# A Strassen matmul with logsumexp: two of eight row tiles taken out of the plain first column block, transposed by DMA instead of PE, and done at the end by seven products

## The chip, the cores and the metric

The kernel runs on one core of one Trainium2 chip. The metric is the device time of one execution in microseconds (us), as the median of several executions. A profile (trace) is one such execution; its span is some 2 us shorter than its time.

Names: PE is the tensor engine, PEld its weight load, DVE the vector engine, ACT the scalar engine, POOL the GpSimd engine, and SP the sync engine, which here only issues DMAs.

## The reference

```python
a = np.random.randn(1024, 4096).astype(np.float32)
b = np.random.randn(4096, 4096).astype(np.float32)

def reference(a, b):
    x = np.matmul(a, b)
    return special.logsumexp(x, axis=-1).astype(np.float32)
```

## The kernel before

The result has 8 row tiles of 128 rows and 8 column blocks of 512 columns. The inputs are cast to f16 by the DMAs that load them.

Column block 0 is done by plain 128x512 products while `a` streams in: PE transposes each 128x128 piece of `a`, DVE and ACT copy the transposes from PSUM (the tensor engine's accumulators) into `aT`, and DVE makes the sums `s1`, `s2`, `s5` of pieces of `a` that Strassen's method needs (called early sums), and two more in place (late sums, `a21-a11` and `a12-a22`), once the plain products have read the originals. Of PSUM's eight tiles, six hold the accumulators of row tiles 0 to 5 and two the transposes, so row tiles 6 and 7 come last. This is the order in which `a` (and, in between, block 0 of `b`) arrives:

```python
    for kn in (4,) * 8:
        ...
        for m in range(MT - 2):                      # row tiles 0 to 5, in rounds of four pieces
            arrivals.append((k0, kn, "a", m))
            if m < kn // 2:
                arrivals.append((k0 + 2 * m, 2, "b", k0))
    for kc in range(KC):
        for m in range(MT - 2, MT):                  # row tiles 6 and 7, after all of the others
            arrivals.append((kc * JT, JT, "a", m))
```

Column blocks 1 to 7 are done by one level of Strassen-Winograd. Two row tiles (a pair `q`) times 512 columns make one "quad" of four 128x256 results and take seven products M1 to M7 of 16 matmuls each, 112 matmuls. Five sums of each block of `b` are made by DVE, called T1, T3, T4, T6, T7. Cut to its core:

```python
            m1(c11, start=True); m5(c12)
            nc.scalar.copy(out=e, in_=r0...)         # r0 is the PSUM tile of c11 and c12
            m2(c21, start=True); m6(c22)
            nc.scalar.copy(out=s[:, 2], in_=c21)
            flush()                                  # exponentials of the quad before
            if tail:                                 # last quad of a block: sums for the next
                for g in range(G):
                    nxt.do_t1(g)
            add(s[:, 2], s[:, 2], e[:, 1])
            sub(s[:, 0], s[:, 2], e[:, 0])
            if final:                                # very last quad
                ...
                combine(0, m0, NB)                   # rows 0-5: the parts of all blocks put together
                sub(lg[:, 0:m0], lg[:, 0:m0], nmmin[:, 0:m0])
                m3(c12)
                nc.scalar.copy(out=x0, in_=c12)
                m4(c21); m7(z, start=True)           # z: the last product
                lse_max(c12, m0, nb); ...            # maxima, exponentials, logarithm, store
                continue
            if tail:
                ...                                  # T6, T3 of the next block
            m7(c11); m3(c12)
            nc.scalar.copy(out=x[:, 0], in_=c12)
            m4(c21)
            nc.scalar.copy(out=x[:, 1], in_=c21)
            ...                                      # results put together
            if tail:
                ...                                  # T4, T7 of the next block
            for h in range(2):
                lse_max(rows[h], 2 * q + h, nb)      # row maxima; exponentials go to the next flush()
```

Of the kernel before, what the change touches and what calls it, by code (L numbers as in the profile page):

```python
# [13 lines left out]
def kernel(  # L14
# [7 lines left out]
    P = 128  # L22
# [13 lines left out]
    SC = 1024  # L36
    KC, JT = K // SC, SC // P
    G = 4
    GI = KP // G
    assert (MT, KT, NB) == (8, 32, 8) and JT == 2 * GI and KC == G  # L40

    a_m = a.rearrange("(p mt) k -> mt p k", mt=MT)

    cst_pool = ctx.enter_context(tc.tile_pool(name="cst", bufs=1))
    bt_pool = ctx.enter_context(tc.tile_pool(name="btp", bufs=2 * G))
    fix_pool = ctx.enter_context(tc.tile_pool(name="fix", bufs=1))
    psum_pool = ctx.enter_context(
# [22 lines left out]
    T1, T4, T6 = tb[:, 0], tb[:, 1], tb[:, 2]  # L70
# [8 lines left out]
    lg = cst_pool.tile([P, MT], f32, name="lg")  # L79

# [47 lines left out]
    def load_b(nb, g, parts=1):  # L128
        bt = bt_pool.tile([P, GI, 2, FD], f16, name=f"b_{nb}_{g}", tag="bt")
        step = 2 * GI // parts  # L130
        flat = bt.rearrange("p i t n -> p (i t) n")
        rows = b.rearrange("(k p) n -> p k n", p=P)
        for h in range(parts):
            nc.gpsimd.dma_start(  # L134
                out=flat[:, h * step : (h + 1) * step],
                in_=rows[:, g * 2 * GI + h * step : g * 2 * GI + (h + 1) * step, ts(nb, FD)],
            )
        return bt

    class Block:  # L140
        def __init__(self, nb):
            self.nb, self.raw = nb, []
# [4 lines left out]
        def rawg(self, g, kp, h):  # L147
            return self.raw[g][:, :, kp, ts(h, H)]

        def do_t1(self, g):  # L150
            add(T1[:, ts(g, GI)], self.rawg(g, 0, 0), self.rawg(g, 1, 1))

        def do_t4(self, g):
            sub(T4[:, ts(g, GI)], self.rawg(g, 1, 0), self.rawg(g, 0, 0))

        def do_t6(self, g):
            add(T6[:, ts(g, GI)], self.rawg(g, 0, 0), self.rawg(g, 0, 1))

        def do_t7(self, g):
            add(self.rawg(g, 1, 0), self.rawg(g, 1, 0), self.rawg(g, 1, 1))  # L160

        def do_t3(self, g):
            sub(self.rawg(g, 0, 1), self.rawg(g, 0, 1), self.rawg(g, 1, 1))
# [5 lines left out]
    blk0 = Block(0)  # L169
# [76 lines left out]
    rounds = []  # L246
    for kn in (4,) * 8:
        k0 = sum(rounds)
        rounds.append(kn)
        for m in range(MT - 2):  # L250
            arrivals.append((k0, kn, "a", m))
            if m < kn // 2:
                arrivals.append((k0 + 2 * m, 2, "b", k0))
    for kc in range(KC):
        for m in range(MT - 2, MT):
            arrivals.append((kc * JT, JT, "a", m))
# [4 lines left out]
    def behind(k0, kn, what, x):  # L261

        if what == "a":
            have_a.setdefault(k0, []).append(x)
            todo = [(k, x) for k in range(k0, k0 + kn) if k in have_b]
        else:
            have_b.update({k0: 1, k0 + 1: 1})
            todo = [(k, m) for k in (k0, k0 + 1) for m in have_a.get(x, [])]
        for k, m in todo:
            if m == MT - 2 and k == 0:  # L270
                acc.append(acc_tiles("l"))
            plain(acc[m // 2][m % 2], k // 2, k % 2, m)
        r = slice(k0 // 2, (k0 + kn) // 2)
        if what == "a" and x < MT - 2:
            if x >= 3 and len(in_place) >= 3:
                a_sums_late(*in_place.pop(0))
            if x % 2 == 1:
                a_sums_early(r, x // 2)
            if x == 5:
                in_place.extend([(r, 0), (r, 1), (r, 2)])  # L280
        if what == "a" and k0 + kn == KT and x in (4, 5):
            first_max(2 * x - 8)
            first_max(2 * x - 7)
        if what == "a" and x >= MT - 2:
            n = 2 * (k0 // JT) + x - (MT - 2)
            if n < 2:
                first_max(4 + n)
            elif in_place:
                a_sums_late(*in_place.pop(0))
# [8 lines left out]
    blk = Block(1)  # L298

    def load(k0, kn, what, x):  # L300
        if what == "a":
            load_a(k0, kn, x)
            return
        if k0 % JT == 0:
            blk0.raw.append(bt_pool.tile([P, GI, 2, FD], f16, name=f"b_0_{k0}", tag="bt"))
        nc.gpsimd.dma_start(  # L306
            out=blk0.raw[k0 // JT][:, k0 % JT // 2],
            in_=b[k0 * P : (k0 + 2) * P, ts(0, FD)].rearrange("(t p) n -> p t n", p=P),
        )

    coming = list(arrivals)
    back = []
    for n, (k0, kn, what, x) in enumerate(arrivals):
        while coming and (coming[0][2] == "b" or loads[0] < count[0] + NSLOT):
            load(*coming.pop(0))
            if len(coming) == len(arrivals) - 3:
                make_identity(nc, ident)
                nc.gpsimd.memset(negmax, 3.0e38)
                nc.gpsimd.memset(tsum, 0.0)
        if not coming and not blk.raw:  # L320
            for g in range(G):
                blk.raw.append(load_b(1, g))
        if what == "a":
            transpose_group(k0, kn, x)
        if k0 < rounds[0] and x < 3:
            warm(1)
        if len(back) == min(3, 1 + n // 8):
            behind(*back.pop(0))
        back.append((k0, kn, what, x))
    while back:  # L330
        behind(*back.pop(0))

    for g in range(G):
        if g == 2:
            for m in range(MT - 2, MT):
                first_max(m)
        for f in (blk.do_t1, blk.do_t6, blk.do_t4, blk.do_t7, blk.do_t3):
            f(g)
# [9 lines left out]
    for nb in range(1, NB):  # L348
        nxt = None
        if nb + 1 < NB:  # L350
            nxt = Block(nb + 1)
            for g in range(G):
                nxt.raw.append(load_b(nb + 1, g))
        quads = {}
        for q in range(MP):
            if q not in quads:

                both = (0, 1) if nb == 1 and q == 0 else (q,)
                for p in both:
                    quads[p] = acc_tiles(f"{nb}_{p}")  # L360
# [4 lines left out]
            def product(c, lhs, rhs, start=False, g=None):  # L365
                for i in range(KP) if g is None else range(g * GI, (g + 1) * GI):
# [9 lines left out]
            first, tail = nb == 1 and q < 2, nxt is not None and q == MP - 1  # L376
            final = nxt is None and q == MP - 1
# [4 lines left out]
            s = fix_pool.tile([P, 4, H], f32, name=f"s_{nb}_{q}", tag="s")  # L382
            x, e = s[:, 1::2], s[:, 0:2]
            if final:
                e = fix_pool.tile([P, 2, H], f32, name=f"e_{nb}_{q}", tag="e")
            if first and q == 1:
                e = e1

            def m1(c, p=q, **k):
                product(c, lambda i: s1[:, i, p], lambda i: T1[:, i], **k)  # L390
# [7 lines left out]
            def m6(c, p=q, **k):  # L398
                product(c, lambda i: aT[:, i, 0, p, 1], lambda i: T6[:, i], **k)
# [7 lines left out]
            def m4(c, **k):  # L407
                product(c, lambda i: aT[:, i, 1, q, 1], lambda i: T4[:, i], **k)

            if first and q == 0:  # L410
                for g in range(G):
                    for p in both:
                        u0, u1 = quads[p]
                        m1(u0[:, 0:H], p=p, start=True, g=g)
                        m5(u0[:, H:FD], p=p, g=g)
                        m2(u1[:, 0:H], p=p, start=True, g=g)
                        m6(u1[:, H:FD], p=p, g=g)
            elif not first:
                m1(c11, start=True)
                m5(c12)  # L420
            if not (first and q == 1):
                nc.scalar.copy(out=e, in_=r0.rearrange("p (h n) -> p h n", h=2))  # L422
            if not first:
                m2(c21, start=True)
                m6(c22, start=final)
            nc.scalar.copy(out=s[:, 2], in_=c21)  # L426
            flush()
            if first and q == 0:
                e1 = fix_pool.tile([P, 2, H], f32, name=f"e_{nb}_1", tag="e")
                nc.scalar.copy(out=e1, in_=quads[1][0].rearrange("p (h n) -> p h n", h=2))  # L430
            if tail:
                for g in range(G):
                    nxt.do_t1(g)
            add(s[:, 2], s[:, 2], e[:, 1])
            sub(s[:, 0], s[:, 2], e[:, 0])
            if final:
# [4 lines left out]
                combine(0, m0, NB)  # L441
                sub(lg[:, 0:m0], lg[:, 0:m0], nmmin[:, 0:m0])
# [30 lines left out]
            if tail:  # L473
                for f in (nxt.do_t6, nxt.do_t3):
                    for g in range(G):
                        f(g)
# [9 lines left out]
            if tail:  # L486
                for f in (nxt.do_t4, nxt.do_t7):
                    for g in range(G):
                        f(g)
# [3 lines left out]
            if first and q == 1:  # L493
                a_sums_early(slice(0, KP), MP - 1)
                a_sums_late(slice(0, KP), MP - 1)
        blk = nxt
# [32 lines left out]
```

## Time and profile before

| | before |
|---|---|
| time | 429.63 us, median of 4 (428.7 to 430.32) when predicting; 429.18 us, median of 15 with later runs |
| span of the profile | 427.1 us |
| PE | 98% busy, 92% of the chain that ended last |
| plain 128x512 product, one after another | 0.216 us |
| 128x128 transpose | 0.055 us |
| 128x256 product | 0.109 us; a quad of 112: 12.225 us |
| first Strassen product starts | 80.11 us |
| last product ends | 422.62 us; 4.48 us before the end |

From the profile page: busy times, the DMA's busy share in 40 slices of the span, and the chain that ended last, by engine.

```profile
PE 418.5 (98%) x3663; PEld 347.9 (81%) x3663; DVE 233.6 (55%) x517; ACT 112.6 (26%) x278; POOL 66.9 (16%) x108
...
DMA  8999999999009900596009910398008930000000
...
PE 92%; DMA 3%; DVE 2%; ACT 1%; issue 1%; POOL 1%; DVEq 0%; ACTq 0%; POOLq 0%
```

The chain is nearly all PE, so a microsecond of PE work should be a microsecond of time. The DMA queues have long idle stretches after the first quarter (the zeros), so there is room for more loading. PE's busy share alone would not be proof: the Trainium skill, "Trainium Kernel Development and Optimization", section "Performance Expectations", calls matmul busy time a bad metric for how close a kernel is to its roofline, because matmuls are pipelined, and names MFU (the share of the peak arithmetic rate that is used) and the busy share of the weight load as the good ones. MFU was not worked out here.

From the timeline of PE, at the change from plain to Strassen products (start, length, engine, line, operation, count).

```profile
72.76 0.61 PE L199 MATMUL tps<-ident,tb 128*128 128x128 f16 x8
73.21 7.07 PE L217 MATMUL acc_l<-b,aT 128*128 128x512 f16 x32
80.11 0.60 PE L367 MATMUL acc<-tb,s 128*128 128x256 f16 x4
```

The plain products of tiles 6 and 7 (`acc_l`) end as the first Strassen product starts. The length of a group includes the pipelined end of its last matmul, so the next group starts a little before the sum of start and length. There is no idle time (it would stand in brackets).

From the timeline of all engines, the last quad.

```profile
405.60 0.43 DVE L82 TENSOR_TENSOR s<-s 128x256 f32<-128x256 f32 x1 [4.10 <-ACT s L426]
...
410.24 1.91 PE L367 MATMUL acc<-tb,s 128*128 128x256 f16 x16
...
416.12 0.42 DVE L82 TENSOR_TENSOR s<-s,e 128x256 f32<-128x256 f32 x1 [2.40 <-ACT s L426]
...
419.57 0.42 DVE L88 TENSOR_REDUCE negmax<-acc 128x1 f32<-128x256 f32 x1 [0.48 <-ACT s L444]
...
420.71 1.91 PE L367 MATMUL z<-b,aT 128*128 128x256 f16 x16
```

The last quad starts at 410.24, and the last product, z, ends at 420.71 + 1.91 = 422.62. DVE has idle time here (4.10 and 2.40 us in brackets): no next block needs sums. The row maximum of C12 starts at 419.57. From there a chain of short operations runs to the end.

### The profile page before, as it was taken

How to read it: one execution, taken by the hardware profiler on the slowest of the kernel's cores; microseconds unless marked ns; L12 is line 12 of the kernel's file. 1: busy time of each engine (PE TensorE's matmuls, PEld its weight loads, DVE VectorE, ACT ScalarE, POOL GpSimd, SP SyncE). 2: the span in 40 equal slices, each digit the busy share in tenths (PEclk: the TensorE clock that was granted, in tenths of full speed). 3: DMA queues.
4: the chain of work that ended last, by engine and by line, in shares of the span. 5: the costliest groups of instructions: out<-in, count | busy, mean ns of one | idle time of the engine just before them, and what ended most of it. 6: DMA issues, size and time to landing. Idle time of an engine off the chain costs nothing.

```text
span 427.1 us, 8496 instructions
## 1 busy us (share of the span) xinstructions
PE 418.5 (98%) x3663; PEld 347.9 (81%) x3663; DVE 233.6 (55%) x517; ACT 112.6 (26%) x278; POOL 66.9 (16%) x108
## 2 busy tenths in 40 slices
PE   7999999999999999999999999999999999999995
PEld 2555565688888888888888888888888888888884
DVE  1456677744789324862369333863359531883235
ACT  1222335112222212222221222222212222222134
POOL 7766752100011000300003000300003000000000
PEclk9999999999999999999999999999999999999999
DMA  8999999999009900596009910398008930000000
GB/s 119 197 203 204 203 208 207 207 207 207 16 0 198 197 3 1 79 207 111 2 0 164 207 27 0 47 207 145 0 2 131 208 57 2 2 2 2 1 2 1
DMA packets 41717, 42.49 MB, mean 99 GB/s; under 512 B 1744, under 2 KB 40656, under 8 KB 41680
## 3 DMA queue, kind: packets, MB, share of 16 engines
q0 software_dynamic: 41536, 41.95, 59.9%
q8 instruction: 28, 0.46, 0.4%
q14 instruction: 9, 0.07, 0.1%
q1 hardware_dynamic: 144, 0.00, 0.0%
HBM read 83.89 MB, written 0.00 MB: 196 GB/s over the span
## 4 chain that ended last, share of the span: by engine, by line
PE 92%; DMA 3%; DVE 2%; ACT 1%; issue 1%; POOL 1%; DVEq 0%; ACTq 0%; POOLq 0%
PE acc L367 79%; PE acc L217 8%; DMA tb<-in_a_dram 3%; PE tps L199 3%; PE acc_l L217 2%; ACT acc L93 0%; DVE negmax L88 0%; PE c L367 0%; DVE aT L85 0%; POOL tb L188 0%; DVE s L82 0%; ACT aT L212 0%; POOL b L306 0%; DVE aT L210 0%; ACT s L467 0%
## 5 line engine op out<-in xcount | busy, mean ns | idle before, releaser
L367 PEld LDWEIGHTS <-aT 128*128 128x128 f16 x1792 | 175.3, 98 | 20.3
L367 PEld LDWEIGHTS <-s 128*128 128x128 f16 x1344 | 131.5, 98 | 15.4
L367 PE MATMUL acc<-tb,aT 128*128 128x256 f16 x880 | 106.0, 273 | 0.0
L367 PE MATMUL acc<-b,s 128*128 128x256 f16 x896 | 103.4, 273 | 0.0
L367 PE MATMUL acc<-b,aT 128*128 128x256 f16 x880 | 100.6, 273 | 0.0
L85 DVE TENSOR_TENSOR s<-s 128x256 f32<-128x256 f32 (+1 forms) x54 | 30.1, 557 | 85.2 <-ACT s L481 84.3
L134 POOL DMA_DIRECT2D b<-in_b_dram x28 | 24.6, 888 | 242.0 <-PE acc L367 226.6
L367 PE MATMUL acc<-tb,s 128*128 128x256 f16 x448 | 54.5, 273 | 0.0
L217 PE MATMUL acc<-b,aT 128*128 128x512 f16 x192 | 49.8, 379 | 0.0
L82 DVE TENSOR_TENSOR s<-s 128x256 f32<-128x256 f32 x26 | 11.0, 422 | 60.3 <-ACT s L426 60.3
L93 ACT ACTIVATE acc<-acc,negmax 128x512 f32<-128x512 f32 (+1 forms) x62 | 40.7, 657 | 5.1 <-DVE negmax L88 4.6
L88 DVE TENSOR_REDUCE negmax<-acc 128x1 f32<-128x512 f32 (+1 forms) x62 | 39.4, 676 | 1.2 <-ACT s L444 0.5
L422 ACT COPY s<-acc 128x512 f32<-128x512 f32 x26 | 15.2, 586 | 87.1 <-PE acc L367 87.1
L82 DVE TENSOR_TENSOR tb<-b 128x1024 f16<-128x1024 f16 x56 | 35.0, 684 | 4.2 <-DMA b<-in_b_dram 4.2
L217 PEld LDWEIGHTS <-aT 128*128 128x128 f16 x256 | 22.7, 98 | 17.5 <-ACT aT L212 0.3
L199 PEld LDWEIGHTS <-tb 128*128 128x128 f16 x256 | 18.8, 99 | 17.7 <-DMA tb<-in_a_dram 5.1
L188 POOL DMA_DIRECT2D tb<-in_a_dram x56 | 30.3, 544 | 8.8 <-PE tps L199 3.1
L212 ACT COPY aT<-tps 128x512 f16<-128x512 f16 (+1 forms) x28 | 18.1, 648 | 48.5 <-PE tps L199 48.5
L426 ACT COPY s<-acc 128x256 f32<-128x256 f32 x28 | 10.4, 372 | 74.8 <-PE acc L367 73.1
L210 DVE COPY aT<-tps 128x512 f16<-128x512 f16 (+1 forms) x28 | 12.9, 462 | 30.4 <-PE tps L199 30.4
L199 PE MATMUL tps<-ident,tb 128*128 128x128 f16 x256 | 23.7, 221 | 2.9 <-DMA tb<-in_a_dram 2.7
L82 DVE TENSOR_TENSOR acc<-acc,s 128x256 f32<-128x256 f32 x54 | 20.6, 428 | 2.7 <-DVE s L85 0.5
(51 smaller groups left out, 173.1 us busy)
## 6 DMA issues: line engine op xcount, KB each, us to landing
b<-in_b_dram POOLq DMA_DIRECT2D x28, 1024.0 KB, 17.0
tb<-in_a_dram POOLq DMA_DIRECT2D x48, 128.0 KB, 5.9
b<-in_b_dram POOLq DMA_DIRECT2D x16, 256.0 KB, 6.2
tb<-in_a_dram POOLq DMA_DIRECT2D x8, 256.0 KB, 7.4
out_dram<-lg SPq DMA_DIRECT2D x1, 4.0 KB, 1.4
```

Source lines behind the costliest of these rows:

```text
L82: nc.vector.tensor_tensor(out=o, in0=x, in1=y, op=ALU.add)
L85: nc.vector.tensor_tensor(out=o, in0=x, in1=y, op=ALU.subtract)
L88: nc.vector.tensor_reduce(out=negmax[:, m, nb : nb + 1], in_=pt, axis=AX.X, op=ALU.max, negate=True)
L93: nc.scalar.activation(out=pt, in_=pt, func=AF.Exp, bias=negmax[:, m, nb : nb + 1], scale=scale, accum_out=tsum[:, m, nb : nb + 1],)
L134: nc.gpsimd.dma_start(out=flat[:, h * step : (h + 1) * step], in_=rows[:, g * 2 * GI + h * step : g * 2 * GI + (h + 1) * step, ts(nb, FD)],)
L188: nc.gpsimd.dma_start(out=slot, in_=a_m[m, :, k0 * P : (k0 + kn) * P])
L199: nc.tensor.matmul(pst[:, ts(j, P)], src[:, ts(j, P)], ident, is_transpose=True, start=(j == 0), stop=(j == kn - 1),)
L210: nc.vector.tensor_copy(out=dst, in_=v)
L212: nc.scalar.copy(out=dst, in_=v)
L217: nc.tensor.matmul(pt, aT[:, i, kp, m // 2, m % 2, :], blk0.raw[i // GI][:, i % GI, kp, :], start=(done[m] == 0), stop=(done[m] == KT - 1),)
L367: nc.tensor.matmul(c, lhs(i), rhs(i), start=(start and i == 0), stop=(i == KP - 1), skip_group_check=True,)
L422: nc.scalar.copy(out=e, in_=r0.rearrange("p (h n) -> p h n", h=2))
```

## The change

The intent: 64 plain products are dearer than one quad (64 x 0.216 = 13.8 us against 12.2 us), and 64 transposes come on top (3.5 us). So row tiles 6 and 7 leave the first stage. They are copied to DRAM in f16, brought into `aT` by two DMA transposes on SP's queue, and block 0 and block 1 of these rows are done at the very end by one quad each ("again0", "again1"), for which both blocks of `b` are loaded once more. Block 1's other three quads are now done jointly, in eighths, as block 1 arrives. A gate, a tiny copy on POOL that reads the transposed data, keeps the load of block 3 from being issued before the transposes have landed. The combination of rows 0 to 5 moves to the quad before the last.

```diff
-    for kc in range(KC):
-        for m in range(MT - 2, MT):
-            arrivals.append((kc * JT, JT, "a", m))
...
+    again0 = lambda: Block(0, sums=[wide(t[:, :, 0:2]) for t in (s1, s2, s5)])
+    again1 = lambda: Block(1, raw=[wide(aT[:, ts(g, GI), :, 0:2]) for g in range(G)])
+    plan = [(lambda: blk1, range(MP - 1))]
+    plan += [(lambda nb=nb: Block(nb), range(MP)) for nb in range(2, NB)]
+    plan += [(again0, [MP - 1]), (again1, [MP - 1])]
...
+                if step == 1:
+                    nc.gpsimd.tensor_copy(out=gate, in_=aT[:, 0, 0, MP - 1, :, 0])
+                nxt = plan[step + 1][0]().load_all()
+        if step == 0:
+            a16 = dram_pool.tile([2, P, K], f16, name="a16")
+            for m in range(2):
+                nc.gpsimd.dma_start(out=a16[m], in_=a_m[MT - 2 + m])
+            for m in range(2):
+                nc.sync.dma_start_transpose(
+                    aT[:, :, :, MP - 1, m, :].rearrange("p i t c -> p (i t) c"), a16[m]
+                )
...
+                for lo in range(0, KP, 2):             # block 1, three quads jointly, by eighths
+                    if lo > 0:
+                        for what in ("t1", "t6"):
+                            blk.make(what, lo, lo + 2)
+                    if lo == KP - 2:
+                        while in_place:
+                            a_sums_late(*in_place.pop(0))
...
+            one = tail and len(qs) == 1
+            if one:
+                nxt.make("t1")
+                combine(0, 2 * q, NB)
+                sub(lg[:, 0 : 2 * q], lg[:, 0 : 2 * q], nmmin[:, 0 : 2 * q])
...
-                combine(0, m0, NB)
-                sub(lg[:, 0:m0], lg[:, 0:m0], nmmin[:, 0:m0])
```

## The prediction

> **What bounds the kernel now.** The tensor engine (PE), back to back. The chain of waits is 92% PE; the PE timeline has no gap between 23.7 us and the last product at 422.6 us. By the page's chain, a plain 128x512 product costs 0.216 us, a 128x128 transpose 0.055, a 128x256 Strassen product 0.109 (one group of 112, a "quad", 12.225 us). From 10.25 us: 256 plain products and 256 transposes until 80.1, then 28 quads x 12.225 = 342 us. A vector/scalar tail of about 4.5 us follows the last product (span 427.1, median 429.63).
>
> **What the change does to PE.** Row tiles 6 and 7 leave column block 0 and are never transposed on PE: 64 plain products (13.8 us) and 64 transposes (3.5 us) go, 17.3 us. One quad comes: 29 instead of 28 (rows 6-7 of block 0 done by seven products at the end). Net 5.1 us less PE work, all on the critical path. That is the whole gain, 1.2%.
>
> **What it gives back.**
> 1. Change-over to block 1. Before, the transposes and products of tiles 6-7 hid the row maxima, exponentials and sums there. Now vector work must finish first. From the timeline at 58-66 us, my estimate: last plain product at 62.4, while the vector engine still has late sums (0.48 us each pair), early sums (0.69), four row maxima (0.64 each) and then the first T1 sum, ready at about 63.7; later PE waits for the last exponentials to free PSUM. About 1.7 us of new PE idleness. Not bound by loads: block 1 no longer queues behind tiles 6-7 (about 10 us of DMA at 207 GB/s), so its eighths arrive from about 60.5 us every 2.5 us, against 2.6 us of PE per eighth.
> 2. Tail. The last step is again preceded by a quad that must make five sums for it (2.5 us each), plus the final combination of rows 0-5. By the durations at 410-424 us, the maxima and exponentials of the quad before then come late, and the scalar copy of the last C12 slips by about 1.5 us; the chain after it is pure latency, so the end slips by 1.5.
>
> **The side path.** Tiles 6-7 go to DRAM as f16 behind block 2, landing at about 106 and 111 us, then two DMA transposes of 1 MiB. The trace of before has none. The Trainium skill, "DMA: Bandwidth & Descriptors", section "Latency and other measured facts", gives 261 GB/s for a transpose with a non-contiguous middle dimension: an estimate of 4 us each. The sums want them by about 128 us and block 3's load, gated on them, by about 124. So I expect no stall, but one transpose over about 9 us would begin to cost, one for one. The reloads of blocks 0 and 1 fall into idle DMA time (the slices show zeros) and cost nothing.
>
> **Sum.** 429.6 - 5.1 + 1.7 + 1.5 = 427.7; I say 427.3, range 424.3 to 431.5. Chance of faster by over 2%: 0.04; within 2%: 0.88; slower by over 2%: 0.08.
>
> **What would show it right or wrong.** Plain products end near 62.4 instead of 73-80 us. The first Strassen product waits on the vector engine for 1-2 us. Last product ends near 419 us; 3,645 or so PE instructions; from there to the end 6 us instead of 4.5. DMA transposes land before 124 us, and PE shows no wait at the fourth quad of block 2 or the first of block 3.
>
> **What would make it wrong.** Slow DRAM writes or transposes (a stall of 5-15 us around 125-150 us, hence the slower chance); a larger stall at the change-over; or the tail's slip being absorbed (then 425).

## The result, and the profile after

| | before | after |
|---|---|---|
| time, median (lowest to highest), executions | 429.18 (428.7 to 430.32), 15 | 426.2 (425.74 to 428.1), 11 |
| ratio | 1 | 0.9933, 95% interval 0.9922 to 0.9944 |
| span of the profile | 427.1 | 424.9 |
| first Strassen product | 80.11 | 64.53 |
| from there to the start of z | 340.60 | 353.37 |
| last product ends | 422.62 | 419.81 |
| from there to the end of the span | 4.48 | 5.09 |

A ratio here is the mean time of one kernel's fast runs over that of the other's of the same rounds, so it is not quite the ratio of the medians quoted. The kernel is faster by 0.7%, which counts as the same time at a limit of 2%.

From the profile page after: the same three lines.

```profile
PE 414.1 (97%) x3647; PEld 348.5 (82%) x3647; DVE 258.1 (61%) x566; ACT 110.1 (26%) x278; POOL 73.3 (17%) x115
...
DMA  8999999999969599003980089300990059599000
...
PE 86%; DVE 7%; DMA 4%; ACT 1%; issue 1%; POOL 1%; DVEq 0%; ACTq 0%; POOLq 0%
```

PE has 16 instructions fewer: 64 products and 64 transposes went, 112 products came. DVE has 24.5 us more to do and a part in the chain, 7%. The new loads near the end fill slices that were zero.

From the timeline of PE and DVE after, at the change from plain to Strassen products.

```profile
59.79 3.62 PE L228 MATMUL acc<-b,aT 128*128 128x512 f16 x16
60.25 0.48 DVE L87 TENSOR_TENSOR aT<-aT 128x256 f16<-128x256 f16 x2
60.65 1.28 DVE L90 TENSOR_REDUCE negmax<-acc 128x1 f32<-128x512 f32 x2
...
62.86 1.28 DVE L90 TENSOR_REDUCE negmax<-acc 128x1 f32<-128x512 f32 x2
64.06 0.75 DVE L84 TENSOR_TENSOR tb<-b 128x512 f16<-128x512 f16 x2
64.53 0.39 PE L383 MATMUL acc<-tb,s 128*128 128x256 f16 x2 [1.12 <-DVE tb L84]
```

Plain products end at 63.41 us. DVE is busy without a break with late sums (L87), row maxima (L90) and early sums (L84, in the lines left out), and only then makes the first T1 (`tb`). PE waits 1.12 us for it.

From the timeline of PE and DVE after, in the first quad of block 2.

```profile
105.11 2.48 DVE L87 TENSOR_TENSOR tb<-b 128x1024 f16<-128x1024 f16 x4
107.51 2.49 DVE L84 TENSOR_TENSOR b<-b 128x1024 f16<-128x1024 f16 x4
108.25 4.15 PE L383 MATMUL acc<-b,aT 128*128 128x256 f16 x32
...
115.73 3.66 PE L383 MATMUL acc<-b,s 128*128 128x256 f16 x32
```

A group of 32 products that is not held up takes 3.66 us (the last line). The group of M7 and M3 at 108.25 took 4.15: its products follow DVE's T7 (L84, group by group) and wait 0.5 us in all. The prediction did not have this wait.

From the timeline of PE and DVE after, the last quad.

```profile
406.00 2.49 DVE L87 TENSOR_TENSOR aT<-aT 128x1024 f16<-128x1024 f16 x4
407.42 1.91 PE L383 MATMUL acc<-tb,s 128*128 128x256 f16 x16
...
412.27 2.49 DVE L84 TENSOR_TENSOR aT<-aT 128x1024 f16<-128x1024 f16 x4
...
414.68 1.28 DVE L90 TENSOR_REDUCE negmax<-acc 128x1 f32<-128x512 f32 x2
...
417.14 0.42 DVE L90 TENSOR_REDUCE negmax<-acc 128x1 f32<-128x256 f32 x1
...
417.90 1.91 PE L383 MATMUL z<-aT 128*128 128x256 f16 x16
```

DVE now makes the five sums for "again1" without a break, and the row maximum of C12 comes 9.72 us after the quad's start (417.14 - 407.42), where it was 9.33. The last product ends at 419.81, and the end follows 5.09 us later instead of 4.48. Of these 0.61 us, 0.39 are the later maximum; the operations from the maximum to the last one of DVE take the same time in both traces, and the other 0.2 us lie behind DVE's last operation (2.6 us instead of 2.4), where only the store of the result is left. Why that is longer was not looked into.

From the DMA issues (name, queue, count, median us from issue to landing), the waits of POOL, and the timeline of POOL, all after: the side path. Each is one view.

```profile
aT<-a SPq DMA_TRANSPOSE x2, 8.5
```

```profile
POOL gate L359 <- DMA aT<-a: 44.7, 1, 44.7
```

```profile
119.37 0.18 POOL L359 COPY gate<-aT 128x2 f16<-128x2 f16 x1 [44.66 <-DMA aT<-a]
119.94 3.54 POOL L144 DMA_DIRECT2D b<-in_b_dram  x4 [0.38 <-issue]
```

The transposes took 8.5 us each from issue to landing (8.7 and 8.2), twice the estimate, and the gate opened at 119.37. No PE wait followed. The moving itself was not slow: between 114 and 117 us, when the second transpose was the only transfer under way, the DMA moved 286 GB/s, at which 1 MiB takes 3.7 us. The rest of the 8.5 us lies before the first byte and after the last, or beside another transfer.

**The ledger.** The start of Strassen moved by -15.58 us: 17.3 us of work removed, 1.12 us of new waiting, and some 0.6 us of waits for the first loads that differ from run to run (below). The stretch from there to z grew by 353.37 - 340.60 = 12.77 us: one quad (12.225) and 0.54 us of waiting. The tail grew by 0.61. So -17.3 + 12.2 + 1.12 + 0.54 + 0.61 = -2.8 us without the loads. With them it is -2.2, as the two profiled spans differ. The medians differ by 3.0.

**The loads.** The last group of plain products starts at 59.79 in this trace, and in those of all ten other runs with the same loads of the first stage (the second run of this kernel, e10, and all of the experiments below but e7) at 58.69 to 60.29, as the waits for the first pieces of `a` come out shorter or longer. That spread of 1.6 us is of the size of the effects sought. So where a fraction of a microsecond matters, the text reads distances inside one execution, which do not contain it.

### The profile page after: what moved, and what is told of

Same layout as the page of the kernel before. It is cut to its first block, busy times and chain, and to the rows that moved or that the text cites. A ratio compares the mean times of both kernels' runs of the same rounds, so it can differ in the third digit from the quotient of the medians.

```text
span 424.9 us, 8520 instructions
## 1 busy us (share of the span) xinstructions
PE 414.1 (97%) x3647; PEld 348.5 (82%) x3647; DVE 258.1 (61%) x566; ACT 110.1 (26%) x278; POOL 73.3 (17%) x115
## 4 chain that ended last, share of the span: by engine, by line
PE 86%; DVE 7%; DMA 4%; ACT 1%; issue 1%; POOL 1%; DVEq 0%; ACTq 0%; POOLq 0%
PE acc L383 78%; PE acc L228 6%; DMA tb<-in_a_dram 3%; PE tps L210 2%; DMA b<-in_b_dram 1%; DVE negmax L90 1%; DVE tb L84 1%; DVE aT L87 1%; DVE s L87 1%; DVE aT L84 1%; DVE tb L87 1%; DVE s L84 0%; DVE acc L84 0%; POOL tb L199 0%; POOL b L144 0%
## 5 line engine op out<-in xcount | busy, mean ns | idle before, releaser
L383 PEld LDWEIGHTS <-s 128*128 128x128 f16 x1392 | 136.1, 98 | 17.4 <-DVE tb L84 1.6
L383 PE MATMUL acc<-tb,aT 128*128 128x256 f16 x880 | 108.5, 273 | 0.0
L144 POOL DMA_DIRECT2D b<-in_b_dram x52 | 41.9, 814 | 222.8 <-PE acc L383 207.8
L87 DVE TENSOR_TENSOR s<-s 128x512 f32<-128x512 f32 (+1 forms) x55 | 30.8, 559 | 74.6 <-ACT s L521 73.5
L84 DVE TENSOR_TENSOR s<-s 128x256 f32<-128x256 f32 x26 | 10.9, 421 | 50.9 <-ACT s L459 50.7
L90 DVE TENSOR_REDUCE negmax<-acc 128x1 f32<-128x512 f32 (+1 forms) x64 | 40.7, 676 | 0.7
L84 DVE TENSOR_TENSOR tb<-b 128x1024 f16<-128x1024 f16 (+1 forms) x64 | 36.1, 617 | 4.9 <-DMA b<-in_b_dram 2.8
L210 PEld LDWEIGHTS <-tb 128*128 128x128 f16 x192 | 14.3, 99 | 16.6 <-DMA tb<-in_a_dram 8.9
L199 POOL DMA_DIRECT2D tb<-in_a_dram x48 | 25.9, 543 | 6.2 <-issue 2.4
L221 DVE COPY aT<-tps 128x512 f16<-128x512 f16 x24 | 10.2, 424 | 25.6 <-PE tps L210 25.4
L223 ACT COPY aT<-tps 128x512 f16<-128x512 f16 x24 | 14.0, 585 | 44.5 <-PE tps L210 44.5
L84 DVE TENSOR_TENSOR acc<-acc,s 128x256 f32<-128x256 f32 x56 | 21.4, 428 | 2.4
L210 PE MATMUL tps<-ident,tb 128*128 128x128 f16 x192 | 18.9, 221 | 3.3 <-DMA tb<-in_a_dram 3.3
```

Of the source, the lines that this page charges most:

```text
L84: nc.vector.tensor_tensor(out=o, in0=x, in1=y, op=ALU.add)
L87: nc.vector.tensor_tensor(out=o, in0=x, in1=y, op=ALU.subtract)
L90: nc.vector.tensor_reduce(out=negmax[:, m, nb : nb + 1], in_=pt, axis=AX.X, op=ALU.max, negate=True)
L144: nc.gpsimd.dma_start(out=self.raw[lo // GI][:, lo % GI : lo % GI + hi - lo], in_=b_rows[:, lo:hi, :, ts(self.nb, FD)],)
L199: nc.gpsimd.dma_start(out=slot, in_=a_m[m, :, k0 * P : (k0 + kn) * P])
L210: nc.tensor.matmul(pst[:, ts(j, P)], src[:, ts(j, P)], ident, is_transpose=True, start=(j == 0), stop=(j == kn - 1),)
```

## The experiments

My theory was the prediction's: the gain is the PE work, minus DVE work that is too late at two places, the change-over and the last quad, to which the trace added the first quad of block 2; the side path is hidden. The rivals: PE work is not worth its time there; the gate or the transposes cost time; the DVE waits are not the cause of what is missing, and something else binds there.

| run | what it is | median us | ratio to before, 95% interval |
|---|---|---|---|
| e1_combine_early | combination one quad earlier | 426.05 | 0.9925 (0.9912 to 0.9937) |
| e2_late_sums_later | last late sums deferred | 425.81 | 0.9917 (0.9904 to 0.9931) |
| e3_block2_sums | two sums of block 2 earlier | 426.2 | 0.9926 (0.9913 to 0.9938) |
| e8_all_three | these three together | 425.55 | 0.9913 (0.99 to 0.9927) |
| e4_dose | 32 more products in the middle | 429.84 | 1.0006 (0.9988 to 1.0025) |
| e5_no_gate | no gate | 432.71 | 1.0077 (1.0058 to 1.0096) |
| e6_late_transposes | transposes later | 434.52 | 1.012 (1.0099 to 1.0142) |
| e7_half | before, with only the quad at the end | 442.8 | 1.0314 (1.0289 to 1.0339) |
| e9_reordered | e8 and a new order of sums and products | 426.86 | 0.9944 (0.9925 to 0.9962) |
| e10_after_again | the change, once more beside e9 | 426.51 | 0.9927 (0.991 to 0.9945) |
| e11_order_m3_m7 | e9 with the products in another order | 424.15 | 0.9892 (0.9876 to 0.9909) |

All results were correct. The kernel before took 429.07 to 429.52 us (medians), so medians can differ by 0.45 us without a cause in the kernel. The intervals of e1, e2, e3 and e8 overlap with that of the change (0.9922 to 0.9944): by time alone none of the four is told from it, and what they show is in the distances below. e11's interval lies clear of it. The distances of the profiled executions, all worked out from the timelines; "to z" is from the start of the first Strassen product to the start of z, and 29 quads without any wait would give 28 x 12.225 + 6/7 x 12.225 = 352.8:

| run | wait at the change-over | to z | from the end of z to the end |
|---|---|---|---|
| after | 1.12 | 353.37 | 5.09 |
| e1_combine_early | 1.12 | 353.38 | 5.08 |
| e2_late_sums_later | 0 | 354.23 | 5.15 |
| e3_block2_sums | 1.12 | 353.07 | 5.15 |
| e8_all_three | 0 | 353.44 | 5.13 |
| e9_reordered | 0 | 355.52 | 4.75 |
| e11_order_m3_m7 | 0 | 352.99 | 4.78 |

### e1_combine_early: is the combination what delays the tail?

```diff
             if one:
                 nxt.make("t1")
-                combine(0, 2 * q, NB)
-                sub(lg[:, 0 : 2 * q], lg[:, 0 : 2 * q], nmmin[:, 0 : 2 * q])
             nc.scalar.copy(out=s[:, 2], in_=c21)
             flush()
+            if early and q == MP - 1:                # one quad earlier
+                combine(0, 2 * q, NB)
+                sub(lg[:, 0 : 2 * q], lg[:, 0 : 2 * q], nmmin[:, 0 : 2 * q])
```

> The changed kernel with one part moved: the final combination of rows 0 to 5 is done one quad earlier, in block 7's last quad, where the vector engine has idle time. Theory (the tail's slip comes from a vector engine that has no idle time from the five sums of the last step to its end): about 1.4 us of vector work and scalar round trips leave that row of work, so the maximum of the last C12 starts about 9.3 us after the last step's first product, as in the kernel before, instead of 9.8; the time from the last product to the end falls from 5.1 to about 4.6 us and the total by about 0.5 us (425.7). Rival (the slip comes from the scalar engine's exponentials of the quad before, or is noise): no change of that distance, total 426.2.

It did not help. From the timeline of DVE in e1_combine_early, from the quad before the last on.

```profile
398.30 2.49 DVE L84 TENSOR_TENSOR tb<-aT 128x1024 f16<-128x1024 f16 x4
402.49 0.42 DVE L84 TENSOR_TENSOR s<-s 128x256 f32<-128x256 f32 x1 [1.70 <-ACT s L457]
...
416.84 0.42 DVE L90 TENSOR_REDUCE negmax<-acc 128x1 f32<-128x256 f32 x1
```

The combination's place in DVE's row is empty now, 1.70 us of idle time: DVE waits for ACT's copy of C21, which waits for PE. The combination had filled a gap of DVE. The last quad starts at 407.13 there, so the maximum at 416.84 comes 9.71 us after it, as in the changed kernel. In the place where the change had put it, the combination is not the cause of the tail's 0.6 us; this part of the theory fell. (What it costs in its old place, in the last quad, e7_half will show.)

### e2_late_sums_later: are the late sums the cause of the change-over wait?

```diff
-            if x >= 3 and in_place:
+            if x >= 3 and in_place and k0 + kn < KT:   # not in the last round
                 a_sums_late(*in_place.pop(0))
...
-                    if lo == KP - 2:
-                        while in_place:
-                            a_sums_late(*in_place.pop(0))
+                    if lo >= 4 and in_place:            # spread over the joint quads instead
+                        a_sums_late(*in_place.pop(0))
```

> The changed kernel with the vector engine's order at the change-over altered: the in-place subtractions that the last round still does before the first sum of block 1 (three pairs, 0.4 us each) are done during block 1's eighths instead. Theory (PE's 1.1 us wait before the first Strassen product is for the vector engine's backlog): the first T1 sum is ready about 1.2 us earlier, the wait shrinks to 0.3 us or less, total falls by about 1 us (425.2). Rival A (the wait is for block 1's data or for PSUM banks): the wait stays, 426.2. Rival B: the wait moves to the third pair of PSUM banks, whose exponentials come later; then less than half of the 1.1 us is won.

The wait of 1.12 us is gone, so it was a wait for DVE's full row, and taking the three pairs of late sums (1.2 us) out of that row was enough. That they more than the row maxima beside them were the cause is not shown: moving these was not tried. Not much was won. From the timeline of PE in e2_late_sums_later, the two waits it has instead.

```profile
93.21 1.91 PE L383 MATMUL acc<-tb,aT 128*128 128x256 f16 x16 [0.23 <-ACT s L458]
...
95.49 3.65 PE L383 MATMUL acc<-b,aT 128*128 128x256 f16 x32 [0.37 <-ACT e L472]
```

PE was earlier and ran into the next thing that was not: DVE, in program order, stood 3.28 us before a T1 of block 2 whose data had not landed (it ran at 89.21), and everything that it does for block 1's results came after that. Of 1.12 us taken away, 0.86 came back before z (354.23 instead of 353.37), so 0.26 stayed in this execution; the medians differ by 0.4.

### e3_block2_sums: is the 0.5 us of block 2 one of order?

```diff
+            if joint and q == 1:                     # T1, T6 of the third group, one quad earlier
+                for what in ("t1", "t6"):
+                    nxt.make(what, 2 * GI, 3 * GI)
...                                                  # and left out of the last quad's list
```

> The changed kernel with two sums (T1 and T6 of block 2's third group, 0.6 us each) done one quad earlier, where the vector engine stands idle for 1.6 us. Theory (PE's wait of 0.5 us inside the first quad of block 2, at 108 us, is for the last in-place sum of B21, at the end of an unbroken row of vector work): that row ends about 1.2 us earlier, the 0.5 us wait goes, total falls by 0.5 us (425.7). Rival (the wait is for something else, or the data of the third group are not there yet and delay the quad): no gain, or a loss.

The group of M7 and M3 is back at 3.66 us, but PE loses 0.24 us at 96.36 instead. The distance to z is 353.07, which is 0.3 us shorter; the median does not show it.

### e8_all_three

This is e1, e2 and e3 in one kernel; it has no other edit.

> The three edits of the runs above together. If the three losses are separate waits of a kernel bound by PE, they add: about 1.1 + 0.5 + 0.5 = 2 us less than the changed kernel, about 424.2, last product near 418.2 us in the profile. If one of them only uncovers another wait, less.

It is 0.65 us faster than the change by the medians, where the sum of the three would have been some 2 us. The change-over wait is gone; 0.37 us of waiting at 95.88 for ACT remains, and the tail is as long as in the changed kernel (5.13 against 5.09). So the DVE waits are real, but moving one of these pieces of work hands its wait to the next one in DVE's fixed order.

### e4_dose: is PE work worth its time?

```diff
             elif not joint:
+                if step == 3 and q == 0:
+                    for _ in range(2):
+                        m1(c11, start=True)          # 32 products whose result is overwritten
                 m1(c11, start=True)
```

> The changed kernel with 32 extra 128x256 products in block 4 (the first seven-product sum is computed three times; the result is unchanged). Theory (PE bound, back to back, so the change's gain is the PE work it removes at face value): 32 x 0.109 = 3.5 us more, about 429.7. Rival (PE is busy by the record but waits for something else in these stages): clearly less than 3.5.

From the timeline of PE in e4_dose: the first Strassen product and z.

```profile
64.00 0.39 PE L383 MATMUL acc<-tb,s 128*128 128x256 f16 x2 [1.13 <-DVE tb L84]
...
420.88 1.91 PE L383 MATMUL z<-aT 128*128 128x256 f16 x16
```

The distance to z grew from 353.37 to 356.88, by 3.51 us for 32 x 0.109 = 3.5, and the median by 3.6. In the steady part (block 4 was tried) a microsecond of PE work is a microsecond of time. A rival that sees another bound there fell.

### e5_no_gate: does the gate cost or save?

```diff
...                                                  # the gate's tile goes too
-                if step == 1:
-                    nc.gpsimd.tensor_copy(out=gate, in_=aT[:, 0, 0, MP - 1, :, 0])
                 nxt = plan[step + 1][0]().load_all()
```

> The changed kernel without the small copy that holds block 3's load back until the DMA transposes have landed. Theory (the side path is off the critical path with some us to spare): total unchanged within 0.5 us; the load of block 3 now runs beside the transposes, so they take longer than their 8.5 us each, by how much is what the run tells; no PE wait at the fourth quad of block 2 unless they land after about 131 us. Rival (the gate guards a transposition that ordinary transfers would slow badly): transposes land after 131 us, a PE wait of several us appears there.

The kernel without the gate is 6.5 us slower than with it (432.71 against 426.2). From three views of e5_no_gate: DMA issues, waits of DVE, and timeline of PE.

```profile
aT<-a SPq DMA_TRANSPOSE x2, 25.6
```

```profile
DVE s L83 <- DMA aT<-a: 11.1, 1, 11.1
```

```profile
141.99 3.22 PE L380 MATMUL acc<-tb,s 128*128 128x256 f16 x16 [3.47 <-DVE s L83]
145.00 4.06 PE L380 MATMUL acc<-b,s 128*128 128x256 f16 x32
148.91 1.91 PE L380 MATMUL acc<-tb,aT 128*128 128x256 f16 x16
```

Beside the load of block 3 a transpose takes 25.6 us from issue to landing (the median of two, 33.1 and 18.1) instead of 8.5. DVE waits 11.1 us for the data, PE 3.47 us for DVE, and then PE is slow for a while: 16 products in 3.22 us instead of 1.91, and 32 in 4.06 instead of 3.66. So the wait cost 3.47 and the slow restart another 1.7; 0.5 more came behind it, at the T7 of block 3. That is 5.7 of the 5.9 us by which the distance to z grew in this execution. The Trainium skill says, in "DMA: Bandwidth & Descriptors", section "Issuing engines are not separate DMA queues", that DMAs of different engines run on the same 16 DMA engines and interleave; that agrees with the trace: the transposes are issued by SP and the load by POOL, and while both were under way (110 to 116 us) the DMA moved 196 GB/s in all, against 290 between 137 and 139 us, at the end of the transposes. The skill's "TensorE: Matmul & The Clock Gate", section "Part 1: The HAM clock gate", says that PE falls to half its clock after an idle window of about 3.4 us; the wait of 3.47 us and the slow products after it agree, and so does the granted clock, 0.60 from 142 to 144 us and 0.54 from 144 to 146.

### e6_late_transposes: how much room has the side path?

```diff
             a16 = dram_pool.tile([2, P, K], f16, name="a16")
+            spare = dram_pool.tile([2, P, K], f16, name="spare")
+            for m in range(2):
+                nc.gpsimd.dma_start(out=spare[m], in_=a_m[m])   # copies that nobody reads, ahead of the real ones
```

> The changed kernel with an unused copy of two other row tiles to DRAM put ahead of the copy of tiles 6 and 7: the transposes come about 10 us later (to land near 129 instead of 119 us) and with them block 3's load. Theory of the prediction (block 3 is wanted by a gate at about 124 us, later costs one for one): PE waits about 5 us at the end of block 2 or the start of block 3, total near 431. Rival (more slack than I thought): less than 2 us.

The gate opened at 128.07 instead of 119.37, so 8.70 us later, and the median rose by 8.3. From the timeline of PE in e6_late_transposes.

```profile
153.46 0.60 PE L386 MATMUL acc<-tb,s 128*128 128x256 f16 x4 [1.81 <-DVE tb L84]
...
163.47 5.21 PE L386 MATMUL acc<-b,aT 128*128 128x256 f16 x32 [4.17 <-DVE b L84]
```

The two waits are 1.81 and 4.17, together 5.98 us, and after the longer one 32 products take 5.21 us instead of 3.66, another 1.55 (granted clock 0.56 to 0.59 between 163 and 167 us). That makes 7.5; the two spans differ by 7.6 (432.5 against 424.9). After the shorter wait there was no slowing: 4 products in 0.60 us, as everywhere. So of 8.70 us of delay 5.98 came through as waiting, and the room was about 2.7 us, an estimate from this one delay. The limit for the gate is then some 122 us, not 124.

### e7_half: is the same PE saving worth the same without the rest of the change?

On the kernel before: block 0 of rows 6 and 7 leaves the plain products and is done by a quad at the end, but they are still loaded and transposed by PE, and block 1 is not done jointly.

```diff
-            if m == MT - 2 and k == 0:
-                acc.append(acc_tiles("l"))
+            if m >= MT - 2:
+                continue                             # no plain products of tiles 6, 7
...
-    for nb in range(1, NB):
+    order = list(range(1, NB)) + [0]
+    for step, nb in enumerate(order):
...
-        for q in range(MP):
+        for q in range(MP) if nb > 0 else [MP - 1]:
```

> The kernel before with only one half of the change: rows 6 and 7 of block 0 are left out of the plain products and done by a quad at the end, but their tiles still come in the first stream of loads and are transposed on PE. By PE work alone (rival): 13.8 us less, 12.2 more, so 1.6 us faster than before, about 427.6. Theory (taking tiles 6 and 7 out of the first stream of loads matters as much as the PE work, since block 1 lands at 73 to 88 us behind them): PE runs dry after about 66 us and waits for block 1, its last quarter still starts at about 89 us, so only about 1 us is won there and the quad at the end is paid in full: about 11 us slower than before, near 440.

By PE's count it should gain 1.6 us (13.8 - 12.2); it lost 13.7 (442.8 against 429.07). From the waits of PE in e7_half, and from its busy times in stretches of 10 us (bounds, length, busy time and count of PE, PEld, DVE, ACT, POOL; then the granted clock, the DMA's share and GB/s).

```profile
PE acc L365 <- DVE tb L82: 4.1, 3, 2.0
PE tps L199 <- ACT aT L212: 3.8, 2, 3.4
```

```profile
60.00:70.00 10.00, 6.55 (x67) 4.87 (x65) 8.30 (x23) 6.19 (x15) 6.63 (x8) 0.92 1.15 207
70.00:80.00 10.00, 7.63 (x49) 5.70 (x48) 7.26 (x17) 1.88 (x2) 0.00 (x0) 0.57 1.24 207
```

The DMA moves 207 GB/s without a break: block 1 comes behind tiles 6 and 7, and PE, which has lost the plain products that covered this, waits for the transposes' copies and for sums of data just landed, 7.9 us in all. The longest wait is 3.38 us, close to the window of about 3.4 us named above, and the granted clock is 0.57 between 70 and 80 us: again the products are slow (4 took 1.01 us instead of 0.60). This wait is not one for loads: ACT had four exponentials to do, from 63.5 us on and in part waiting for DVE's maxima, before the copy at 67.61 that PE needed. The last product ends 10.7 us later than before (433.36), and the tail is 6.5 us. From the timeline of PE and DVE in e7_half, the last quad.

```profile
420.97 1.91 PE L365 MATMUL acc<-tb,s 128*128 128x256 f16 x16
...
432.41 0.42 DVE L88 TENSOR_REDUCE negmax<-acc 128x1 f32<-128x256 f32 x1
```

The maximum of C12 comes 11.44 us after the quad's start: behind the five sums, the combination of rows 0 to 5 takes DVE from 430.61 to 432.32, just before it. So the count of PE work explains the change only together with its other parts: rows 6 and 7 leave the load path in front of block 1, block 1 is done in eighths, and the combination moves one quad ahead. How much the first two and the order of ACT's work do at the change-over, these runs do not separate.

### e9_reordered and e10_after_again: the sums and products in another order

From e8's failure I took that DVE's order has to change as a whole. On e8, with the part of e3 put in another form: only the first group of block 2 is prepared after the first joint quad, T1 and T6 of its second group after the second, T6 for "again1" is made straight after T1, and the products are issued as M3, M4, M7, to give T7 more time. e10 is the changed kernel once more beside it on the same chip.

```diff
...                                                  # the order of block 2's sums
             if one:
                 nxt.make("t1")
+                nxt.make("t6")
...
-            m7(c11)
             m3(c12)
             nc.scalar.copy(out=x[:, 0], in_=c12)
             m4(c21)
             nc.scalar.copy(out=x[:, 1], in_=c21)
+            m7(c11)
```

> A second version, after the run with three edits won only half of the 2 us hoped for. Its edits: (1) the last round's in-place sums of A during block 1's eighths, as before; (2) of block 2's early sums only those of the first group stay ahead of the first quad's correction, the second group's come one quad later, so that the vector engine no longer stands waiting for the second group's data while PE waits for it; (3) in each quad the products run in the order M3, M4, M7 instead of M7, M3, M4, so that the last-made sum is wanted last; (4) the combination of rows 0-5 in block 7's last quad and T6 of the last step right after its T1, where the vector engine otherwise waits. Theory (each loss is a wait of PE or of the tail for the vector engine): no PE wait between 60 and 150 us, the last product ends about 1.6 us earlier than in the changed kernel, the tail falls from 5.1 to about 4.6 us; total about 424.1. Rival (the stage is bound by the loads of blocks 1 and 2 as much as by the vector engine): PE waits for sums of block 2 remain and at most 1 us is won, about 425.2.

> The changed kernel itself, unaltered, for comparison on the same chip: about 426.2 us, 0.993 of the kernel before.

The change-over wait, the 0.5 us in block 2 and the late maximum are all gone: the maximum of C12 comes 9.34 us after the quad's start (before: 9.33), and the tail is 4.75. (Before it was 4.48; what is left lies behind DVE's last operation, as in the changed kernel.) But nothing was won in time, because of a new wait. From the timeline of DVE, ACT and PE in e9_reordered.

```profile
109.75 1.28 DVE L90 TENSOR_REDUCE negmax<-acc 128x1 f32<-128x512 f32 x2
...
111.81 0.37 ACT L521 COPY s<-acc 128x256 f32<-128x256 f32 x1
...
112.23 1.91 PE L383 MATMUL acc<-b,aT 128*128 128x256 f16 x16 [1.98 <-ACT s L521]
```

M7 (the last line) adds into C11. It waited 1.98 us for ACT's copy of C12 (L521). C11 and C12 are the two halves of one PSUM tile, and this copy stands in ACT's row behind two exponentials, which wait for DVE's row maxima (L90). e10 showed the waits of the changed kernel again (1.13 us at the change-over, 4.15 us for the group of M7 and M3).

### e11_order_m3_m7: is that wait one of the products' order?

```diff
             m3(c12)
+            m7(c11)
             nc.scalar.copy(out=x[:, 0], in_=c12)
             m4(c21)
             nc.scalar.copy(out=x[:, 1], in_=c21)
-            m7(c11)
```

> As e9_reordered, but the products in the order M3, M7, M4, and the scalar copy of C12 issued after M7. If the 1.98 us wait of e9 at 112 us came from M7 overwriting half of a PSUM tile whose other half was still to be copied, that wait is gone here, the stage from the first Strassen product to the last product z is about 2 us shorter than e9's 357.4 minus the changed start, and the median is about 424.7 (424.2 to 425.2). Rival: the stage of blocks 1 and 2 is bound by the loads and the vector engine, so a wait of like size turns up elsewhere before 115 us and the median stays at 425.5 or above.

424.15 us (423.71 to 425.52), the fastest of all, and a little under the expectation. The whole list of PE's waits in e11_order_m3_m7:

```profile
PE tps L210 <- DMA tb<-in_a_dram: 2.7, 4, 1.0
PE acc L290 <- DVE s L293: 1.2, 1, 1.2
```

These are the first loads and the very first product, which waits in every kernel here. The wait of 1.98 us is gone and the stretch to z is 352.99 us, 2.53 less than in e9 and 0.2 from the 352.8 of an unbroken row (one group of 32 products still takes 3.81 us instead of 3.66). As the products' order is the only difference between e9 and e11 (with it, the copy of C12 is now issued behind M7), it was the cause; and the rival, that loads and DVE bind this stage and the wait would come back elsewhere, fell. Against the change, e11 has 1.12 us less at the change-over, 0.38 less to z and 0.31 less in the tail, together 1.8; the medians differ by 2.05, and the ratios by 0.0041, which is 1.8 us. Within 2% of the kernel before it still is, at 1.1% faster.

## Why the prediction was right

It said 427.3 us (424.3 to 431.5), most likely within 2%. The median was 426.2, inside that range and 1.1 us below its point. Point by point:

1. **What bounds the kernel: right.** e4_dose shows it: 3.5 us of added products cost 3.51 us to z.
2. **PE work, -5.1 us: right.** The start of Strassen moved by 17.3 us less what is named in points 3 and 6, and the part after it by one quad plus 0.54 us.
3. **Change-over, +1.7: the cause right, the size 1.12.** The wait had the form foretold ("The first Strassen product waits on the vector engine for 1-2 us"), and e2_late_sums_later showed that it goes when the late sums leave DVE's row. What the estimate put on top, a second wait "for the last exponentials to free PSUM", did not come. The wait turned out not to be simply there for the taking: moved away alone, most of it came back 30 us later.
4. **A wait in block 2's first quad, +0.5: not foreseen.** DVE's row between 96.6 and 109.9 us has no gap, and T7 comes too late there.
5. **Tail, +1.5: the cause half right, the size 0.6.** The five sums before the last quad do delay the maximum of C12, but by 0.4 us (9.72 against 9.33 us after the quad's start). The other 0.2 us lie behind DVE's last operation and stay open. That the combination adds to the slip was wrong for this kernel: the change had moved it into a gap of DVE, and moving it further won nothing (e1_combine_early). Left in the last quad it does add to it: in e7_half the maximum comes after 11.44 us and the tail is 6.5. The prediction counted as a cost what the change itself avoids. With T6 made straight after T1, in e9 and e11, the tail was 4.75 and 4.78; that it was this edit out of the several in those kernels is argued and was not run alone.
6. **Loads: said to be no limit; right for block 1,** whose joint quads ran without a wait. The first stage had about 0.6 us more waits for the first pieces of `a` in the profiled execution, a thing that varies by 1.6 us from one execution to the next.
7. **The side path, no stall: right, with less room than thought.** The step "an estimate of 4 us each" failed: the transposes took 8.5 us from issue to landing. The rate was not at fault (286 GB/s when one ran alone); the estimate left out the time before the first byte and after the last. "Block 3's load ... by about 124" was some 2 us too generous: e6_late_transposes puts the limit near 122. What was left at 119.37 was about 2.7 us. And the warning "a stall of 5-15 us around 125-150 us" if the transposes were slow is what e5_no_gate showed when the gate is away: PE waited 3.47 us at 142 us, and the time rose by 6.5 us, the slow restart included. The prediction took the gate as a dependency with a deadline; it did not see that the gate earns its place by keeping the transposes clear of the load.

So the mechanism held, and that the sum came so near has luck in it: two terms were too high (0.6 and 0.9), one of 0.5 was missing, the starting time of 429.6 was 0.4 above the later median, and the point of 427.3 had been set 0.4 below the prediction's own sum of 427.7.

## What to carry to other kernels

When PE is the bound, price a change by PE work first, then look for the places where another engine's fixed order of work is overtaken by the earlier PE; each such wait is small, and taking one away alone mostly moves it to the next late piece (e1, e2 and e3 won 0 to 0.4 us each, within the noise), while ordering the whole row won 2 (e11). Keep DMA transposes clear of bulk loads, do not price them by their rate alone, and check how long a wait may get before PE's clock falls: 1.8 and 2.0 us of waiting cost just that, and waits of 3.5 and 4.2 us cost 1.55 to 1.7 more. Before reordering products, see which of them share a PSUM tile with a result that another engine still has to copy.

## What the Trainium skill lacked or had wrong

- "DMA: Bandwidth & Descriptors", section "Latency and other measured facts", states 261 GB/s for a DMA transpose with a non-contiguous middle dimension, and "Advanced Engine Details and Errata", section "X-Bar Transpose (TRN2)", expects 350-400 GB/s. The rate here lay between the two: 286 GB/s from 114 to 117 us, when the second transpose ran alone. What these two places do not give is the time around it: 1 MiB took 8.7 and 8.2 us from issue to landing, so an estimate from the rate alone, 4.0 us at 261 GB/s, was too short by a factor of two.
- "DMA: Bandwidth & Descriptors", the rules for kernel authors, says that a transpose next to ordinary DMAs needs nothing. The result was correct in e5_no_gate, as that rule has it, but no page that I read gives the cost in time: 8.5 us became 25.6 beside the load of a block.
- "TensorE: Matmul & The Clock Gate", section "Part 1: The HAM clock gate", gives the idle window of about 3.4 us, and the runs agree. What one such gap costs in a running kernel has to be worked out from it; here it was, beyond the gap, 1.7 us after 3.47 us and 1.55 us after 4.17 us. After gaps of 1.81 us and 1.98 us the next products ran at the usual speed.
- "Trainium Kernel Development and Optimization", section "Performance Expectations", names the busy share of the weight load, beside MFU, as a good measure of how close a kernel is to its roofline. For comparing two versions it was too coarse here: it rose from 81% to 82% and could not show a gain of 3 us in 429.
- A figure that belongs to "PSUM — Partial Sum Buffer": what it costs when a product into one half of a PSUM tile waits for another engine's copy of the other half. It was 1.98 us in e9_reordered, and nothing in e11_order_m3_m7, with another order. Whether the chip asks for this wait or only the way the kernel's dependencies are tracked, no run here tells.
